# First block of a two-block network: latents' squares taken from PSUM as they are projected, state space outputs transposed per channel block over all eight steps

## The chip, the cores and the metric

The kernel runs on one core of a Trainium2 chip. Its five engines are TensorE (PE, with its weight loads PEld), VectorE (DVE), ScalarE (ACT), GpSimd (POOL) and SyncE (SP), which here only issues DMAs. The metric is the device time of one execution in microseconds; lower is better.

## What is computed

Two blocks run one after the other on 1024 tokens of width 1024. Only the first block is touched by the change. Cut to what matters:

```
x = layer_norm(x)                                   # [1024 tokens, 1024]
z = x @ w_in
xs, gs, cq, ckv, kr, gm = split(z, 512, 512, 256, 128, 64, 512)
ys = s5_branch(xs, ...) * silu(gs)                  # state space model, 32 groups of 16 channels, 64 states
       # y = gelu(scan output + d_skip * xs);  y = y * sigmoid(y @ w_glu + b_glu)
ym = mla_branch(cq, ckv, kr, ...) * silu(gm)        # 4 heads of causal attention
       # q = rms_norm(cq) @ w_uq;  k_nope, v = rms_norm(ckv) @ w_ukv;  rotary on the last 64 of q and on kr
mix = concat(ys, ym) @ w_out
u = alpha * x + mix;  x = layer_norm(u + sigmoid(u @ w_pg) * (p @ w_pp))
```

cq (256 wide) and ckv (128 wide) are the latents. Their RMS norms need, for each token, the sum of squares over the latent's channels. The second block is a dilated attention, a gated linear recurrence and a mixture of 32 experts.

## The kernel before, in words

All matrix products are made in float32 out of three float32r products (high x high, high x low, low x high): `mm3` at L178 to L180, called by `gemm`. A split into high and low is a ScalarE copy (L146, or L150 with a scale) and a VectorE subtraction (L147, L153). `evac` copies a PSUM tile to SBUF, alternating between ScalarE (L139) and VectorE (L141).

The kernel is written with a tile framework. The program text gives instructions in an order of emission; a scheduler at compile time puts them into the queues of the engines, taking whichever is ready in its plan, by the order of emission where several are. On the chip each engine then works through its own queue in order.

`block1` (from L272) begins with the layer norm; x is transposed to xTh and xTl. Then three streams are emitted interleaved by `weave` (L396). Each stream yields its costs as it goes, and `weave` always advances the stream whose sum of costs, divided by the number given with it, is the smallest. The streams:
- `s5_prep` (L774), which makes the state space parameters (costs 84 in all, mostly VectorE work on 128x512 tiles; tables of cosines and sines go to DRAM as d_cos and d_sin, L894 and L895), then `s5_groups` (L899): eight turns over four groups each (8.0 each, 64 in all). A turn makes Q1 on GpSimd and X1p on VectorE (L921 to L923), transposes X1p (L940), runs two input products (L968), a scan on VectorE (L974), output products (L984 to L986, 24 matmuls a turn) and a gelu (L991 to L995), whose result goes to s5y: 128 partitions (blocks of eight tokens), then step t within the block, then 512 channels. The number given is 148.
- The projections x @ w_in: eight chunks of 256 columns, each in four tiles (two column blocks, two halves of the tokens) of 24 matmuls of 128x512, with cost 5.2 each, 32 tiles in all. Results lie channel by token. `g_xs` (L334) handles xs. `g_feat` (L369) handles the latents and the rotary key (copied by `evac` to a tile co, stored to d_c in DRAM at L377) and then the gates gs and gm (`silu2`: a tanh on ScalarE, L331, and a product on VectorE, L332). The number given is 166.4.
- `rest`, then `latent_norms` (L347), then `rotary_tables` (L380); the number given is 180.

`latent_norms` loads each of the six latent tiles (two of cq and one of ckv, in two halves) back from d_c into co (L356), squares it on ScalarE (L357), and sums over the channels on TensorE with four matmuls against a column of ones (L359, eight instructions in the profile). VectorE combines the sums (L364 to L366) and takes the reciprocal root c.lr.

PSUM has eight banks; in this part four tiles G (projections) and four tiles T (all others) of one bank each.

`mla` (L469) comes next. It changes PSUM to G=3, T=3, P=2 and weaves `prep` and `glu`:
- `prep` (L491) loads the latents (ct, L494) and the rotary key (kr, rt) from d_c, broadcasts c.lr by transposes into P (L507), multiplies on VectorE (L510), splits into cnh and cnl, and rotates the key (L487 to L489, L515, L516).
- `glu` (L435) loads the stored gates (gs, L446). For each of the eight steps t it transposes the four 128-channel pieces of s5y into one T tile (L450), splits it into yh and yl at the columns t, t+8, t+16 and so on, and multiplies gs at the same columns (L452). Then eight tiles of y @ w_glu follow (12 matmuls of 128x512 each), each with a tanh (L462) and a product y (L464), stored to DRAM.

After that come the first head's projections (`project`), then attention.

Of the kernel before, what the change touches and what calls it, by code (L numbers as in the profile page):

```python
# [11 lines left out]
FT = mybir.dt.float32  # L12
FR = mybir.dt.float32r
I32 = mybir.dt.int32
AF = mybir.ActivationFunctionType
OP = mybir.AluOpType
# [6 lines left out]
NT = 8  # L23
# [248 lines left out]
def block1(c):  # L272

    tc, nc, I = c.tc, c.nc, c.I
    d = c.dram
    d_xln = c.d_xln = d.tile([S, D], FT, name="d_xln")
    d_c = c.d_c = d.tile([512, S], FT, name="d_c")
# [11 lines left out]
    es1 = ExitStack()  # L289
# [3 lines left out]
    xT = lambda k, sl: (xTh[k // 4][:, k % 4, sl], xTl[k // 4][:, k % 4, sl])  # L293
# [40 lines left out]
    def g_xs(n):  # L334
        w = ch.next()
        for mb in range(2):
            o = stage.tile([128, 8, 128], FT, name="xo")
            for i, h in enumerate(half):
                ps = c.ps()
                c.gemm(ps, [(cols(w[k], mb), xT(k, h)) for k in range(8)])  # L340
                c.evac(o[:, :, 64 * i:64 * i + 64], ps.rearrange("p (n t) -> p t n", t=8))
                yield 5.2
            for g in range(8):
                b, gg = divmod(16 * n + 8 * mb + g, 4)
                nc.scalar.dma_start(d_xu[b, :, gg, :].rearrange("(t c) n -> c t n", t=8), o[16 * g:16 * g + 16])

    def latent_norms():  # L347

        c.lr = c.con.tile([128, 2 * NT], FT, name="lr")
        v = c.sm([128, 2 * NT], name="lv")  # L350
        for i, js in enumerate(((0, 1), (2,))):
            for h in half:
                ps = c.psum_tile("T", [128, 4 * len(js)])
                for j in js:
                    o = stage.tile([128, 512], FT, name="co")
                    nc.sync.dma_start(o, d_c[j * 128:j * 128 + 128, h])  # L356
                    nc.scalar.activation(o, o, AF.Square)  # L357
                    for k in range(4):
                        nc.tensor.matmul(ps[:, 4 * j % 8 + k:4 * j % 8 + k + 1], o[:, k * 128:k * 128 + 128], c.cst[:, 20:21],  # L359
                                         start=True, stop=True)  # L360
                    yield 10.0
                d = v[:, i * NT + h.start // 128:i * NT + h.start // 128 + 4]
                if i == 0:
                    nc.vector.tensor_copy(d, ps[:, 0:4])  # L364
                    nc.vector.tensor_add(d, d, ps[:, 4:8])
                nc.vector.tensor_scalar(d, d if i == 0 else ps, 1.0 / (256, 128)[i], 1e-6, op0=OP.mult, op1=OP.add)  # L366
        c.rsqrt(c.lr, v)

    def g_feat(dst, r0, op):  # L369
        w = ch.next()  # L370
        for h in half:
            for mb in range(2):
                ps = c.ps()
                c.gemm(ps, [(cols(w[k], mb), xT(k, h)) for k in range(8)])
                o = stage.tile([128, 512], FT, name="co")
                op(o, ps)
                nc.sync.dma_start(dst[r0 + mb * 128:r0 + mb * 128 + 128, h], o)  # L377
                yield 5.2

    def rotary_tables():  # L380
        pos = stage.tile([128, S], I32, name="ang", tag="xo")
        k = stage.tile([128, S], FT, name="rk", tag="xo")
        nc.sync.dma_start(pos, bcast_rows(I["positions"], S))
        ang = pos.bitcast(FT)
        nc.vector.tensor_scalar(ang, pos, c.cst[:, 18:19], None, op0=OP.mult)
        yield 4.0
        for h in half:
            c.sincos(stage, ang[:, h], 512, c.rsin[:, h], c.rcos[:, h], "rp", r=ang[:, h], k=k[:, h])
            yield 8.0

    def rest(cost):
        yield cost

    gate = lambda o, ps: silu2(o, ps, 512)

    weave((seq(s5_prep(c, es1), s5_groups(c, es1)), 148.0),  # L396
          (seq(g_xs(0), g_xs(1), g_feat(d_c, 0, c.evac), g_feat(d_c, 256, c.evac),
               g_feat(d_gs, 0, gate), g_feat(d_gs, 256, gate), g_feat(d_gm, 0, gate), g_feat(d_gm, 256, gate)), 166.4),
          (seq(rest(100.0), latent_norms(), rotary_tables()), 180.0))
    wg = ch.next(), ch.next()  # L400
    es1.close()

# [8 lines left out]
def seq(*gens):  # L411
    for g in gens:
        yield from g
# [21 lines left out]
def glu(c, p, w):  # L435

    nc, I = c.nc, c.I
    d_ys = c.d_ys = c.dram.tile([512, S], FT, name="d_ys")
    yh = p.tile([128, 4, S], FR, name="yh")
    yl = p.tile([128, 4, S], FR, name="yl")  # L440
    bg = p.tile([128, 4], FT, name="bg")
    nc.sync.dma_start(bg, I["b_glu"].rearrange("(j p) -> p j", p=128))
    nc.vector.tensor_scalar(bg, bg, 0.5, None, op0=OP.mult)
    gs = p.tile([128, 4, S], FT, name="gs")
    for kb in range(4):
        nc.sync.dma_start(gs[:, kb], c.d_gs[kb * 128:kb * 128 + 128, :])  # L446
    for t in range(8):
        ps = c.psum_tile("T", [128, 4, 128])
        for kb in range(4):
            nc.tensor.transpose(ps[:, kb, :], c.s5y[:, t, kb * 128:(kb + 1) * 128], c.ident)  # L450
        c.split(yh[:, :, t::8], yl[:, :, t::8], ps, scale=0.5)
        nc.vector.scalar_tensor_tensor(gs[:, :, t::8], ps, 0.5, gs[:, :, t::8], op0=OP.mult, op1=OP.mult)  # L452
        yield 0.9
    for mb in range(4):
        for h in range(2):
            hs = slice(h * 512, h * 512 + 512)
            cs = slice((mb % 2) * 128, (mb % 2) * 128 + 128)
            ps = c.ps()
            c.gemm(ps, [((w[mb // 2][k][0][:, cs], w[mb // 2][k][1][:, cs]), (yh[:, k, hs], yl[:, k, hs]))
                        for k in range(4)])  # L460
            th = p.tile([128, 512], FT, name="th", bufs=2)
            nc.scalar.activation(th, ps, AF.Tanh, bias=bg[:, mb:mb + 1], scale=0.5)  # L462
            y = p.tile([128, 512], FT, name="y", bufs=2)
            nc.vector.scalar_tensor_tensor(y, th, 1.0, gs[:, mb, hs], op0=OP.add, op1=OP.mult)  # L464
            nc.sync.dma_start(d_ys[mb * 128:mb * 128 + 128, hs], y)
            yield 2.6


def mla(c, ym, ess, wg):  # L469
# [21 lines left out]
    def prep(q):  # L491
        ct = q.tile([128, 3, S], FT, name="ct")
        for j in range(3):
            nc.sync.dma_start(ct[:, j], c.d_c[j * 128:(j + 1) * 128, :])  # L494
        gq = q.tile([128, 3], FT, name="gq")
        nc.sync.dma_start(gq[:, 0:2], I["q_norm_g"].rearrange("(j p) -> p j", p=128))
        nc.sync.dma_start(gq[:, 2:3], I["kv_norm_g"].rearrange("(j p) -> p j", p=128))
        kr = q.tile([128, S], FT, name="kr")
        nc.sync.dma_start(kr, c.d_c[384:512, :])
        swapped(c.d_c[384:512, :], slice(0, S), nc.sync)  # L500
        yield 0.1
        for i in range(2):
            for h in range(2):
                psb = c.psum_tile("P", [128, 4, 128])
                for mm in range(4):
                    k = i * NT + h * 4 + mm
                    nc.tensor.transpose(psb[:, mm, :], c.lr[:, k:k + 1].to_broadcast([128, 128]), c.ident)  # L507
                hs = slice(h * 512, h * 512 + 512)
                for j in ((0, 1) if i == 0 else (2,)):
                    nc.vector.scalar_tensor_tensor(ct[:, j, hs], ct[:, j, hs], gq[:, j:j + 1],  # L510
                                                   psb.rearrange("p a b -> p (a b)"), op0=OP.mult, op1=OP.mult)
                    c.split(cnh[:, j, hs], cnl[:, j, hs], ct[:, j, hs])
                yield 1
        rotary(kr, slice(0, S))
        nc.vector.tensor_copy(kst[0], kr)  # L515
        nc.vector.tensor_sub(kst[1], kr, f32(kst[0]))  # L516
        yield 1

    with ExitStack() as es2:
        q = c.pool(es2, "mlap")  # L520
        c.psum(G=3, T=3, P=2)
        tc.swap_default_side()
        gp = c.pool(ess, "glu")
        tc.swap_default_side()
        weave((prep(q), 5.0), (glu(c, gp, wg), 28.0))
    ess.close()
    p = c.pool(es, "mlah")
    msk = p.tile([128, 128], FT, name="mskf")
# [471 lines left out]
def weave(*streams, first=False):  # L1000

    st = [[g, t, 0.0] for g, t in streams]
    lead = st[0]
    while st and not (first and lead not in st):
        s = min(st, key=lambda a: a[2] / a[1])
        try:
            s[2] += next(s[0])
        except StopIteration:
            st.remove(s)


class Chunks:
# [9 lines left out]
    def next(self):  # L1022
        self.n += 1
        self.ahead(self.n + 1)
        w, self.w[self.n - 1] = self.w[self.n - 1], None
        return w
# [957 lines left out]
```

## Time and profile before

| | us |
|---|---|
| median of 3 runs | 2118.1 |
| lowest, highest | 2114.16, 2118.48 |
| the profiled execution's own time | 2120.2 |
| its span, first to last instruction | 2118.4 |
| its mean granted TensorE clock | 0.951 |

How to read the profile. All times are from the span's start. A row of the windows gives the stretch, its length, then busy time of PE, PEld, DVE, ACT and POOL with the number of instructions, the granted TensorE clock (1.00 is full), the mean busy share of the DMA engines, and GB/s. A row of the timeline gives start, duration, engine, line, operation and operands, and in brackets how long the engine sat idle before it and what ended that wait. Matmul durations overlap: consecutive ones start closer together than they last. A row of the waits reads "who <- for whom: total, times, longest". A row of the groups ends with busy time, mean duration in ns, and the idle time before. The page by 40 slices of 53 us shows the first block in the slices up to about the 14th; the experts fill the last third.

### The profile page before, as it was taken

What the parts mean: (1) busy time and instruction counts of PE and PEld (TensorE: products, weight loads), DVE (VectorE), ACT (ScalarE), POOL (GpSimd) and SP (SyncE); (2) the same over time, 40 slices, a digit from 0 to 9 for tenths busy, and PEclk for the clock granted to TensorE, in tenths of its full rate; (3) what the DMA queues carried; (4) which work ended last, traced back from release to release, by engine and by line L of the source; (5) the groups of instructions that cost most, each with busy time, mean ns of one, the idle gap of its engine ahead of it and who ended that gap; (6) DMA issues with size and microseconds to landing.
All of it is one profiled execution on the core that took longest, in us unless ns stands there. A gap on an engine that the chain in (4) does not pass through costs nothing.

```text
span 2118.4 us, 34587 instructions
## 1 busy us (share of the span) xinstructions
PE 1937.1 (91%) x13242; PEld 1717.9 (81%) x13242; DVE 1498.3 (71%) x2912; ACT 1030.6 (49%) x1580; POOL 311.9 (15%) x241
## 2 busy tenths in 40 slices
PE   2998995899999979999999999999799999999992
PEld 2776884788999979899999898898688888888881
DVE  7387666676334795757457455668999999999995
ACT  3223333444122234545333223235688888888883
POOL 3014320100000000010010000013322222222211
PEclk9899996999999999999999998899899999999996
DMA  4444533310313131111111011356899999999984
GB/s 172 108 130 146 148 101 122 93 56 31 129 37 110 51 109 46 49 51 46 48 45 45 26 36 35 141 199 235 293 368 376 380 371 372 351 364 367 362 305 169
DMA packets 144374, 350.72 MB, mean 166 GB/s; under 512 B 33888, under 2 KB 87776, under 8 KB 119632
## 3 DMA queue, kind: packets, MB, share of 16 engines
q1 hardware_dynamic: 128160, 325.38, 42.9%
q0 software_dynamic: 11152, 19.97, 3.9%
q10 hardware_dynamic: 4896, 3.15, 0.7%
q8 instruction: 105, 1.72, 0.3%
q14 instruction: 61, 0.50, 0.1%
HBM read 305.81 MB, written 54.01 MB: 170 GB/s over the span
## 4 chain that ended last, share of the span: by engine, by line
PE 38%; issue 24%; DVE 10%; POOL 5%; DMA 3%; ACT 2%; SPq 0%; POOLq 0%; DVEq 0%; ACTq 0%
PE psG L178 8%; PE psG L179 8%; PE psG L180 8%; POOL gates L1840 3%; PE psT L1278 2%; PE psPO L1229 2%; PE psPO L1362 1%; POOL xg L1840 1%; PE psPO L613 1%; PE psSC L1208 1%; PE psSC L1209 1%; DVE Sc L1348 1%; PE psSC L1340 1%; POOL d_acc L1933 1%; DMA wraw<-w_in 1%
## 5 line engine op out<-in xcount | busy, mean ns | idle before, releaser
L1875 DVE TENSOR_TENSOR el<-raw,eh 128x1024 fp32r<-128x1024 f32 x384 | 446.2, 1218 | 32.8 <-ACT eh L1874 31.9
L1874 ACT ACTIVATE eh<-raw 128x1024 fp32r<-128x1024 f32 x384 | 396.0, 1059 | 63.8 <-PE psUU L180 24.4
L178 PE MATMUL psG<-aTh,wh 128*128 128x256 f32 x640 | 188.2, 294 | 0.0
L180 PE MATMUL psG<-aTh,wl 128*128 128x256 f32 x640 | 184.3, 288 | 0.6 <-DVE wl L147 0.6
L179 PE MATMUL psG<-aTl,wh 128*128 128x256 f32 x640 | 184.5, 288 | 0.0
L146 ACT ACTIVATE wh<-wraw 128x512 fp32r<-128x512 f32 (+1 forms) x148 | 91.6, 624 | 187.0 <-PE psG L180 77.2
L178 PE MATMUL psG<-wh,aTh 128*128 128x256 f32 x512 | 147.4, 288 | 0.0
L147 DVE TENSOR_TENSOR wl<-wraw,wh 128x512 fp32r<-128x512 f32 (+1 forms) x148 | 104.9, 716 | 58.9 <-ACT wh L146 48.2
L179 PE MATMUL psG<-wl,aTh 128*128 128x256 f32 x512 | 146.3, 286 | 0.0
L180 PE MATMUL psG<-wh,aTl 128*128 128x256 f32 x512 | 145.6, 284 | 0.0
L178 PEld LDWEIGHTS psG<-aTh,wh 128*128 128x128 f32 x640 | 124.6, 195 | 4.8 <-issue 3.9
L180 PEld LDWEIGHTS psG<-aTh,wl 128*128 128x128 f32 x640 | 124.3, 194 | 2.7 <-issue 1.4
L179 PEld LDWEIGHTS psG<-aTl,wh 128*128 128x128 f32 x640 | 124.7, 195 | 1.4 <-issue 0.9
L180 PE MATMUL psG<-xTh,wl 128*128 128x512 f32 x256 | 105.1, 411 | 3.7 <-DVE wl L147 3.7
L178 PE MATMUL psG<-xTh,wh 128*128 128x512 f32 x256 | 105.6, 413 | 0.4 <-ACT wh L146 0.4
L178 PE MATMUL psY<-eh,hh 128*128 128x512 f32 x256 | 102.3, 400 | 1.7 <-ACT hh L150 1.7
L179 PE MATMUL psG<-xTl,wh 128*128 128x512 f32 x256 | 103.8, 405 | 0.0
L178 PE MATMUL psUU<-eh,xh 128*128 128x512 f32 x256 | 102.6, 401 | 0.0
L178 PE MATMUL psGG<-eh,xh 128*128 128x512 f32 x256 | 101.1, 395 | 0.7 <-ACT xh L146 0.7
L179 PE MATMUL psY<-el,hh 128*128 128x512 f32 x256 | 100.2, 391 | 1.0 <-DVE el L1875 1.0
L180 PE MATMUL psGG<-eh,xl 128*128 128x512 f32 x256 | 100.9, 394 | 0.0
L179 PE MATMUL psGG<-el,xh 128*128 128x512 f32 x256 | 100.3, 392 | 0.0
(539 smaller groups left out, 5305.7 us busy)
## 6 DMA issues: line engine op xcount, KB each, us to landing
raw<-w_gate SPq DMA_DIRECT2D x64, 1024.0 KB
raw<-w_down SPq DMA_DIRECT2D x64, 1024.0 KB
raw<-w_up SPq DMA_DIRECT2D x63, 1024.0 KB
wraw<-w_in SPq DMA_DIRECT2D x52, 256.0 KB
wraw<-w_in SPq DMA_DIRECT2D x68, 128.0 KB
wraw<-w_out SPq DMA_DIRECT2D x32, 256.0 KB
x<-x SPq DMA_DIRECT2D x8, 512.0 KB
d_xln<-x SPq DMA_DIRECT2D x8, 512.0 KB
```

The costliest lines, as they stand in the source:

```text
L146: nc.scalar.activation(h, src, AF.Copy)
L147: nc.vector.tensor_sub(l, src, f32(h))
L178: mm(ps, ah, bh, start=first, stop=False)
L179: mm(ps, ah, bl, start=False, stop=False)
L180: mm(ps, al, bh, start=False, stop=last)
L613: mm(po, v[:, k, :], et[k // 4][:, k % 4, :], start=k == 0, stop=k == qb)
L1208: nc.tensor.matmul(sc[:, ks], QS[j][:, qs], KH[j][:, ks], start=True, stop=False)
L1229: nc.tensor.matmul(po[64 * j:64 * j + 64], v[:, k, (b % 2) * 128 + 64 * j:(b % 2) * 128 + 64 * j + 64], et[j][:, i, :], start=k == 0, stop ...
L1278: nc.tensor.transpose(ps[:, i, :], e[:, (k0 + i) * 128:(k0 + i + 1) * 128], c.ident)
L1840: c.nc.gpsimd.indirect_dma_start(out=dst, out_offset=None, in_=src, in_offset=bass.IndirectOffsetOnAxis(ap=idx, axis=0), bounds_check=src. ...
L1874: nc.scalar.activation(h, src, AF.Copy)
L1875: nc.vector.tensor_sub(l, src, f32(h))
```

## The change

1. The squares of the latents are taken when they are projected. A new generator `g_latents` replaces `g_feat` for the two chunks with d_c. It copies every tile by VectorE, and for the three latent column blocks ScalarE squares the PSUM tile into the tile `th`; the four matmuls against ones for a tile are emitted behind the next tile's projection. The sums are kept in `lv`. `latent_norms` no longer loads or squares anything; it adds the two parts of cq, scales, and takes the root.
2. In the first weave, the number of the state space stream goes from 148 to 160, `rest` from 100 to 120, and the rotary tables come before the norms.
3. `glu` transposes one channel block kb at a time, all eight steps, into a PSUM tile T2 of two banks. yh, yl and gs are written densely; PSUM is read with the steps innermost.
4. PSUM in that part is G=2, T2=2 (two banks each), P=2. `glu` is emitted up to the end of its four blocks before `prep` begins; the rest is woven with 5 and 20.

```
+    lv = c.con.tile([128, 3, NT], FT, name="lv")
+    def squares(j, h, sq):
+        ps = c.psum_tile("T", [128, 4])
+        for k in range(4):
+            nc.tensor.matmul(ps[:, k:k + 1], sq[:, k * 128:k * 128 + 128], c.cst[:, 20:21], start=True, stop=True)
+        nc.vector.tensor_copy(lv[:, j, h * 4:h * 4 + 4], ps)
+    def g_latents(js):
+        w = ch.next()
+        late = None
+        for i, h in enumerate(half):
+            for mb, j in enumerate(js):
+                ps = c.ps()
+                c.gemm(ps, [(cols(w[k], mb), xT(k, h)) for k in range(8)])
+                o = stage.tile([128, 512], FT, name="co")
+                nc.vector.tensor_copy(o, ps)
+                if late:
+                    squares(*late)
+                    late = None
+                if j < 3:
+                    sq = stage.tile([128, 512], FT, name="th", bufs=1)
+                    nc.scalar.activation(sq, ps, AF.Square)
+                    late = j, i, sq
+                nc.sync.dma_start(d_c[j * 128:j * 128 + 128, h], o)
+                yield 5.2
+        if late:
+            squares(*late)
     def latent_norms():
...
-                    nc.sync.dma_start(o, d_c[j * 128:j * 128 + 128, h])
-                    nc.scalar.activation(o, o, AF.Square)
...
+        nc.vector.tensor_add(v[:, :NT], lv[:, 0], lv[:, 1])
+        nc.vector.tensor_scalar(v[:, :NT], v[:, :NT], 1.0 / 256, 1e-6, op0=OP.mult, op1=OP.add)
+        nc.vector.tensor_scalar(v[:, NT:], lv[:, 2], 1.0 / 128, 1e-6, op0=OP.mult, op1=OP.add)
+        yield 1.0
         c.rsqrt(c.lr, v)
+        yield 1.0
...
-    weave((seq(s5_prep(c, es1), s5_groups(c, es1)), 148.0),
-          (seq(g_xs(0), g_xs(1), g_feat(d_c, 0, c.evac), g_feat(d_c, 256, c.evac),
+    weave((seq(s5_prep(c, es1), s5_groups(c, es1)), 160.0),
+          (seq(g_xs(0), g_xs(1), g_latents((0, 1)), g_latents((2, 3)),
...
-          (seq(rest(100.0), latent_norms(), rotary_tables()), 180.0))
+          (seq(rest(120.0), rotary_tables(), latent_norms()), 180.0))
...
-    for t in range(8):
-        ps = c.psum_tile("T", [128, 4, 128])
-        for kb in range(4):
-            nc.tensor.transpose(ps[:, kb, :], c.s5y[:, t, kb * 128:(kb + 1) * 128], c.ident)
-        c.split(yh[:, :, t::8], yl[:, :, t::8], ps, scale=0.5)
-        nc.vector.scalar_tensor_tensor(gs[:, :, t::8], ps, 0.5, gs[:, :, t::8], op0=OP.mult, op1=OP.mult)
-        yield 0.9
+    yield 0
+    for kb in range(4):
+        ps = c.psum_tile("T2", [128, 8, 128])
+        for t in range(8):
+            nc.tensor.transpose(ps[:, t, :], c.s5y[:, t, kb * 128:(kb + 1) * 128], c.ident)
+        ps = ps.rearrange("p t n -> p n t")
+        v = lambda a: a[:, kb].rearrange("p (n t) -> p n t", t=8)
+        c.split(v(yh), v(yl), ps, scale=0.5)
+        nc.vector.scalar_tensor_tensor(v(gs), ps, 0.5, v(gs), op0=OP.mult, op1=OP.mult)
+        yield 1.8
...
-        c.psum(G=3, T=3, P=2)
+        c.psum(G=2, T2=2, P=2)
...
-        weave((prep(q), 5.0), (glu(c, gp, wg), 28.0))
+        turn, pre = glu(c, gp, wg), prep(q)
+        for _ in range(5):
+            next(turn)
+        weave((pre, 5.0), (turn, 20.0))
```

More of the change, by code (lines that the diff above doesn't have):

```diff
@@ L350, in latent_norms @@
         v = c.sm([128, 2 * NT], name="lv")
[L351 to L355, printed above, removed]
-                    nc.sync.dma_start(o, d_c[j * 128:j * 128 + 128, h])
[L357 to L366, printed above, removed]
+        nc.vector.tensor_add(v[:, :NT], lv[:, 0], lv[:, 1])
+        nc.vector.tensor_scalar(v[:, :NT], v[:, :NT], 1.0 / 256, 1e-6, op0=OP.mult, op1=OP.add)
+        nc.vector.tensor_scalar(v[:, NT:], lv[:, 2], 1.0 / 128, 1e-6, op0=OP.mult, op1=OP.add)
+        yield 1.0
         c.rsqrt(c.lr, v)
+        yield 1.0
     def g_feat(dst, r0, op):
```

## The prediction

> **What bounds the kernel now.** I read the page first, then busy time in stretches of 10 us, then the waits, and last the order of the instructions between 60 and 400 us, the only part that the change touches.
>
> ```profile
> PE 1937.1 (91%) x13242; PEld 1717.9 (81%) x13242; DVE 1498.3 (71%) x2912; ACT 1030.6 (49%) x1580; POOL 311.9 (15%) x241
> ```
> ```profile
> 160.00:170.00 10.00, 10.00 (x46) 8.29 (x45) 9.66 (x12) 5.23 (x8) 10.00 (x9) 1.00 0.49 158
> 180.00:190.00 10.00, 4.46 (x15) 3.88 (x16) 3.08 (x6) 3.06 (x4) 0.00 (x0) 0.56 0.54 175
> 340.00:350.00 10.00, 3.11 (x12) 2.14 (x12) 9.59 (x12) 2.98 (x4) 0.00 (x0) 0.50 0.00 0
> 350.00:360.00 10.00, 6.02 (x16) 4.07 (x17) 8.76 (x9) 2.93 (x3) 0.00 (x0) 0.50 0.00 0
> ```
>
> The columns after the stretch are its length, then PE, PEld, DVE, ACT and POOL busy, the granted clock, and DMA. Over the span TensorE is the bound (91%). There are two holes in it: 180 to 190 us, where TensorE is busy less than half and every other engine less than a third, and 340 to 360 us, where VectorE is full and TensorE stands at clock 0.50. The change works on both. Who is waited for:
>
> ```profile
> PE psT L359 <- ACT co L357: 12.3, 3, 9.3
> PE psT L450 <- DVE gs L452: 10.1, 3, 7.9
> ```
>
> The first row is the column sums of the latents' squares, waiting for ScalarE, which squares a tile read back from DRAM. The second is the transposes of the state space outputs, waiting for PSUM buffers that VectorE frees.
>
> **The stage of projections and state space: terms.**
>
> ```profile
> 185.54 1.87 PE L359 MATMUL psT<-cst,co 128*128 128x1 f32 x8 [9.32 <-ACT co L357]
> ...
> 275.35 1.05 PE L359 MATMUL psT<-cst,co 128*128 128x1 f32 x8 [1.84 <-ACT co L357]
> ```
> ```profile
> 186.00:188.00 2.00, 2.00 (x9) 1.90 (x10) 0.29 (x1) 0.00 (x0) 0.00 (x0) 0.50 0.59 175
> 188.00:190.00 2.00, 2.00 (x7) 1.52 (x6) 0.01 (x1) 0.60 (x1) 0.00 (x0) 0.50 0.00 0
> 190.00:192.00 2.00, 2.00 (x7) 1.61 (x6) 1.27 (x2) 0.51 (x1) 0.00 (x0) 0.65 0.23 88
> ```
> ```profile
> 276.00:278.00 2.00, 2.00 (x12) 1.71 (x12) 1.51 (x6) 1.05 (x3) 1.26 (x3) 0.69 0.83 260
> 278.00:280.00 2.00, 2.00 (x7) 1.09 (x6) 1.08 (x4) 0.58 (x2) 0.00 (x0) 0.50 0.88 247
> ```
>
> Removed: the six loads of co from d_c, and with them the 12.3 us of TensorE's waits. After the long wait the clock stays low although TensorE is busy: (1-0.50)x2 twice and (1-0.65)x2 make 2.7 us lost; after the short one (1-0.69)x2 and (1-0.50)x2 make 1.6. Sum of the removed: 12.3+4.3 = 16.6 us. By the Trainium skill ("TensorE: Matmul & The Clock Gate", What's actually happening) the full clock is back after about 3.4 us of steady work; by that the first loss would be 1.7 us instead of 2.7.
>
> The squares themselves stay: six groups of matmuls at 1.05 us (the second row at full clock) move forward among the first sixteen projections. Each is queued behind the next projection's 24 matmuls, so ScalarE has 5.4 us to square a tile:
>
> ```profile
> 104.01 0.39 PE L178 MATMUL psG<-xTh,wh 128*128 128x512 f32 x1
> ...
> 109.45 0.39 PE L178 MATMUL psG<-xTh,wh 128*128 128x512 f32 x1
> ```
>
> The two rows are the first matmuls of k and k+8, so one projection tile takes 5.44 us. The square itself costs ScalarE about as much as the tanh row below (0.60 us) and replaces the square in SBUF: nothing on the path. Its one buffer is shared with the gates' tanh, so a square waits for the sums of the one before, which TensorE has done by then; behind it on ScalarE stand the splits of weights, which are a chunk ahead. The rotary tables only change their place in the order, and their work on VectorE is the same.
>
> Added to VectorE: all eight latent tiles are now copied by it, four of them before by ScalarE, and six small copies.
>
> ```profile
> L141 DVE COPY xo<-psG 128x512 f32<-128x512 f32 x4 | 2.8, 691 | 29.0 <-PE psG L180 28.9
> L141 DVE COPY co<-psG 128x512 f32<-128x512 f32 x4 | 2.7, 680 | 0.0
> L364 DVE COPY lv<-psT 128x4 f32<-128x4 f32 x2 | 0.3, 163 | 7.0 <-PE psT L359 7.0
> ```
>
> 4x0.68+6x0.16 = 3.7 us, at a place where VectorE is full (9.66 of 10 us). It delays the parameters of the state space, and X1p of its first group:
>
> ```profile
> 182.49 0.68 DVE L921 TENSOR_TENSOR X1p<-er,KB 128x512 f32<-128x512 f32 x1
> ```
>
> X1p takes three such operations, so it could stand at 184.5 us now and at 188.2 with the additions. The new weight of that stream (160 for 148) puts the first group behind 84/160x32 = 16.8, so 17 projections, instead of 84/148x32 = 18.2, so 19. TensorE began its long wait at 185.54-9.32 = 176.2 us; two projections earlier (-10.9) and six groups of sums later (+6.3) it would come to the first group at about 172 us and wait 16 us, with fifteen projections queued behind. That is the wait that can take the removed one's place. It shrinks where the scheduler moves projections ahead of a transpose that is not ready, and it does such things:
>
> ```profile
> 325.13 0.49 PE L450 MATMUL psT<-ident,s5y 128*128 128x128 f32 x3
> ...
> 325.46 0.49 PE L507 MATMUL psP<-ident,lr 128*128 128x128 f32 x3
> ```
>
> Of four transposes of one step three run, then those of another stream, emitted later. So the wait lies between 0 and 16 us plus a low clock behind it (up to 3). I take 7.5, somewhat under the middle, because three projections fill the whole of it.
>
> The end of the stage:
>
> ```profile
> 315.15 0.60 ACT L331 ACTIVATE th<-psG 128x512 f32<-128x512 f32 x1 [2.60 <-PE psG L180]
> ...
> 324.68 0.39 PE L985 MATMUL psT<-Q,A 128*128 128x128 f32 x2
> ...
> 324.90 0.39 PE L986 MATMUL psT<-Q,A 128*128 128x128 f32 x2
> ...
> 328.12 0.63 ACT L995 ACTIVATE s5y<-yq 128x512 f32<-128x512 f32 x1 [0.76 <-DVE yq L994]
> ```
>
> The last projection ends at 315.15; the last group's 24 output matmuls (2 in 0.22 us, so 2.7) and its gelu then run alone until 328.75. With the stream emitted ahead, (1-148/160)x32 = 2.4 projections follow it and cover that tail. Last projection in the changed kernel: 315.15-16.6+2.7+7.5 = 308.7 us, between 301 and 320.
>
> **The glu stage: terms.**
>
> ```profile
> 382.00 0.69 DVE L464 SCALAR_TENSOR_TENSOR y<-th,gs 128x512 f32<-128x512 f32 x1 [0.15 <-ACT th L462]
> ```
>
> From the last projection to the end of this last product: 382.69-315.15 = 67.5 us now. VectorE's work in it:
>
> ```profile
> L153 DVE SCALAR_TENSOR_TENSOR yl<-psT,yh 128x512 fp32r<-128x512 f32 x8 | 8.8, 1094 | 2.8 <-ACT yh L150 2.8
> L452 DVE SCALAR_TENSOR_TENSOR gs<-psT,gs 128x512 f32<-128x512 f32 x8 | 8.5, 1090 | 0.0
> L510 DVE SCALAR_TENSOR_TENSOR ct<-ct,gq,psP 128x512 f32<-128x512 f32 x6 | 4.2, 751 | 0.0
> L147 DVE TENSOR_TENSOR cnl<-ct,cnh 128x512 fp32r<-128x512 f32 x6 | 3.9, 697 | 0.0
> L489 DVE TENSOR_TENSOR kr<-kr,rt 128x1024 f32<-128x1024 f32 x1 | 1.2, 1232 | 0.0
> ```
> ```profile
> L150 ACT ACTIVATE yh<-psT 128x512 fp32r<-128x512 f32 x8 | 8.4, 1106 | 9.3 <-PE psT L450 8.7 <-DMA rt<-d_c 0.6
> ```
>
> yl and gs write (gs also reads) with a stride of 8 elements and take 1.09 us for 512 where others take 0.70. Now the writes are dense and the reads from PSUM have a stride of 128 elements over two banks. The nearest row for strided PSUM reads is xo above (stride 8): 691 ns against 680 dense, so free. I take 1.23 us for 1024 elements (the kr row; ScalarE 1.1), with 2.18 as the upper end, the strided price of today. By the Trainium skill ("PSUM — Partial Sum Buffer", Specifications) PSUM has 8-byte cachelines and any non-contiguous pattern slows matmuls significantly; taken over to these reads it speaks against the change, and xo's row does not bear it out.
>
> The second gain is the order: a block now carries one contraction chunk for all tokens, so the first glu matmuls need block 0 and not all eight steps. From the last projection: its tanh and product 1.3; eight transposes at
>
> ```profile
> 350.99 1.09 PE L450 MATMUL psT<-ident,s5y 128*128 128x128 f32 x4 [1.38 <-DVE gs L452]
> ```
>
> 0.27 each, 2.1; yh 1.1; yl 1.2: block 0 is done at +5.8. With two buffers, blocks 2 and 3 wait for gs of blocks 0 and 1, with all glu matmuls queued behind: gs0 +7.0, gs1 +9.5, transposes +11.6, yh +12.7, yl of block 3 at +13.9. Then 0.7 for the first tile's last chunk, seven tiles of half a projection (7x2.72 = 19.0), sixteen transposes of the norms among them (1.8 at 0.11, 4.3 at 0.27 each; I take 2.7), 2 for a low clock, the last tanh and product 1.4: +40. VectorE also does the preparation's products; in the trace
>
> ```profile
> 331.51 1.40 DVE L510 SCALAR_TENSOR_TENSOR ct<-ct,gq,psP 128x512 f32<-128x512 f32 x2
> ...
> 333.81 1.30 DVE L147 TENSOR_TENSOR cnl<-ct,cnh 128x512 fp32r<-128x512 f32 x2
> ```
>
> they came between the first yl. I add 4, hence 44, between 40 and 53 (all 8.1 of ct and cnl and the four of kr, at most 4.9, first). The gate loads now stand ahead of the latents' loads on SP, so gs should be there in time; if not, the two buffers hold everything up, within the same 13 us. One PSUM buffer less for the glu tiles costs nothing while a tanh (0.6) is shorter than a tile (2.7).
>
> Last product: 308.7+44 = 352.7 instead of 382.7, 30 us earlier. Nothing after it waits for a clock time, so the rest shifts. The profiled execution took 2120.2 us, 2.1 over the median, so 2090 by its own time and **2088** for the median.
>
> **Rivals.**
> - TensorE never waits at the first group (last projection at 301): 345, a gain of 38: 2080. For it: the scheduler goes by readiness. Against it: VectorE is late in fact, not in its plan.
> - VectorE keeps the old order, or the strided reads cost 2.18: +53: 361.7, a gain of 21: 2097.
> - No change: the last projection at 320 (the 16 us wait with its low clock), and of the second stage only the dense writes count, 8.8+8.5-8x1.23 = 7.5 of the 67.5 us: 320+60 = 380, a gain of 3: 2115. For it: VectorE is full in both stages. Against it: the covered tail and the order of blocks would both have to fail.
> - Slower: the reads over two banks pay at every element. The place is the eight VectorE reads of 1024, today 1.2 ns an element. It decides from 30/(8x1.024) = 3.7 ns more, 4.9 in all. At 8 ns: 8x1.024x6.8 = 56 us more, less 30: 2144. Against it: no strided row here passes 2.2 ns.
>
> **How the numbers follow.** About 0.2% (4 us, the three runs' spread) can be told from no change. Chances: forecast 0.52, never waiting 0.14, old order 0.20, no change 0.06, slower 0.08; faster is the sum of the first three, 0.86. Low end: 301+40, gain 41.7, with 4 for the spread: 2072. High end: 320+53, gain 9.7, and the same 4: 2112.
>
> **What would show it.** Right: no wait for a square on TensorE; the last tanh of the projections near 309; y's last product near 353; VectorE's yl and gs near 1.23 us; the first glu matmul before the last yl. Wrong: a new long wait at the first group's transposes (L940's place) reaching to 190 us or beyond; yl over 2.2 us; the last product after 375.

## The result, and the profile after

The changed kernel takes 2081.96 us (median of 4 runs, 2080.49 to 2087.04) beside 2116.24 us for the kernel before in the same measurement: a ratio of 0.9841, 95% interval 0.9823 to 0.986, or 34.3 us less. The forecast was 2088 (30 us less), with 2072 to 2112 as its range. The profiled execution took 2080.49 us, with a span of 2078.7. From here on "before" and "after" are the two kernels, and lines behind L345 are numbered as in after: the glu stage's transposes L450 are now L470, its gs L452 is L474, its y L464 is L486; X1p L921 to L923 is L946 to L948, its transposes L940 are L965, the output matmuls L984 to L986 are L1009 to L1011, the last gelu L995 is L1020. The squares' sums are L353, the latents' copies L364, the norms' transposes L529 and their products L532.

First the page's busy times, then the stretches that answer to those of before, then TensorE's waits between 60 and 370 us.

```profile
PE 1922.5 (92%) x13242; PEld 1705.7 (82%) x13242; DVE 1487.3 (72%) x2909; ACT 1023.7 (49%) x1572; POOL 316.5 (15%) x241
```
```profile
140.00:150.00 10.00, 10.00 (x35) 8.32 (x35) 9.70 (x22) 3.12 (x5) 1.35 (x1) 0.56 0.54 159
...
180.00:190.00 10.00, 10.00 (x46) 8.29 (x45) 6.67 (x20) 4.35 (x6) 0.00 (x0) 1.00 0.30 102
190.00:200.00 10.00, 5.35 (x24) 3.76 (x23) 6.54 (x12) 3.84 (x8) 4.05 (x4) 0.66 0.74 223
...
310.00:320.00 10.00, 5.52 (x45) 5.02 (x45) 4.13 (x6) 4.90 (x8) 0.00 (x0) 0.97 0.70 223
...
340.00:350.00 10.00, 10.00 (x47) 8.10 (x46) 7.87 (x13) 3.96 (x7) 0.00 (x0) 1.00 0.47 160
```
```profile
PE psT L965 <- DVE X1p L948: 4.7, 1, 4.7
PE psG L178 <- ACT yh L150: 4.5, 1, 4.5
...
PE psG L180 <- DVE wl L147: 2.7, 1, 2.7
...
PE psT L353 <- ACT th L370: 0.2, 1, 0.2
```

The 12.3 us of waits for squares have become 0.2, and in 340 to 350 us TensorE is full at clock 1.00 where it had 3.11 of 10 us at 0.50. Two smaller holes stand in their place: one for X1p at 190 us, one for yh at 310 us. A third loss shows only in the clock: from 140 to 150 us TensorE is busy throughout, at a mean clock of 0.56. Before had 0.99 there:

```profile
140.00:150.00 10.00, 10.00 (x42) 7.28 (x41) 9.90 (x17) 4.78 (x8) 2.54 (x2) 0.99 0.73 253
```

Both kernels wait here for VectorE's wl (2.73 us until 139.56 in after, 2.35 until 136.90 in before) and go on at half clock. In before that lasts 3.2 us, in after 9.2, so some 3 us more are lost. In after two groups of the squares' sums, matmuls with a single column, run within the first 5 us of the stretch. Of the runs further down, the six with two groups of sums in that place have 8.7 to 10.0 us of half clock there, those with one or none 3.2 to 7.1. That the sums keep the clock low fits all of these; no run changes that alone.

The hole at 190 us in the timeline, with the clock in steps of 2 us:

```profile
190.13 0.69 DVE L946 TENSOR_TENSOR X1p<-er,KB 128x512 f32<-128x512 f32 x1
190.73 0.68 DVE L332 SCALAR_TENSOR_TENSOR co<-th,psG 128x512 f32<-128x512 f32 x1
191.33 0.69 DVE L147 TENSOR_TENSOR wl<-wraw,wh 128x512 fp32r<-128x512 f32 x1
192.88 0.68 DVE L940 TENSOR_TENSOR dg<-dg,ident 16x512 f32<-16x512 f32 x1 [0.86 <-DMA dg<-d_skip]
...
194.79 0.69 DVE L948 TENSOR_TENSOR X1p<-X1p,ctmp 128x512 f32<-128x512 f32 x1
```
```profile
195.63 1.09 PE L965 MATMUL psT<-ident,X1p 128*128 128x128 f32 x4 [4.65 <-DVE X1p L948]
```
```profile
196.00:198.00 2.00, 2.00 (x11) 1.29 (x10) 0.69 (x1) 1.15 (x3) 1.92 (x2) 0.50 0.71 202
198.00:200.00 2.00, 2.00 (x10) 1.59 (x9) 1.26 (x3) 0.59 (x1) 1.71 (x3) 0.50 0.88 219
200.00:202.00 2.00, 2.00 (x15) 1.83 (x15) 1.77 (x5) 0.00 (x0) 0.49 (x2) 1.00 0.73 162
```

TensorE waits 4.65 us, then works at half clock from 195.6 to 200: 2.2 us more. In before, too, dg and its load stood between X1p's operations, and the last one came at 192.76:

```profile
185.61 0.68 DVE L915 TENSOR_TENSOR dg<-dg,ident 16x512 f32<-16x512 f32 x1 [2.44 <-DMA dg<-d_skip]
...
192.76 0.68 DVE L923 TENSOR_TENSOR X1p<-X1p,ctmp 128x512 f32<-128x512 f32 x1
```

So X1p is complete 2.0 us later than before, though its first operation starts 7.6 us later. The second hole, ScalarE's rows first, then TensorE's, then VectorE's:

```profile
309.80 0.60 ACT L331 ACTIVATE th<-psG 128x512 f32<-128x512 f32 x1 [2.53 <-PE psG L180]
313.92 0.63 ACT L146 ACTIVATE wh<-wraw 128x512 fp32r<-128x512 f32 x1 [3.53 <-DMA wraw<-w_uq]
314.46 0.58 ACT L1016 ACTIVATE yq<-psT 128x512 f32<-128x512 f32 x1
...
317.29 0.63 ACT L1020 ACTIVATE s5y<-yq 128x512 f32<-128x512 f32 x1 [0.75 <-DVE yq L1019]
317.82 1.92 ACT L150 ACTIVATE yh<-psT 128x1024 fp32r<-128x1024 f32 x2
```
```profile
312.05 0.39 PE L1011 MATMUL psT<-Q,A 128*128 128x128 f32 x2
312.27 1.91 PE L470 MATMUL psT<-ident,s5y 128*128 128x128 f32 x16
...
318.88 0.49 PE L178 MATMUL psG<-yh,wh 128*128 128x512 f32 x1 [4.48 <-ACT yh L150]
```
```profile
318.86 1.23 DVE L153 SCALAR_TENSOR_TENSOR yl<-psT,yh 128x1024 fp32r<-128x1024 f32 x1 [1.61 <-ACT yh L150]
...
328.42 1.22 DVE L153 SCALAR_TENSOR_TENSOR yl<-psT,yh 128x1024 fp32r<-128x1024 f32 x1
329.55 1.21 DVE L474 SCALAR_TENSOR_TENSOR gs<-psT,gs 128x1024 f32<-128x1024 f32 x1
```
```profile
349.95 0.69 DVE L486 SCALAR_TENSOR_TENSOR y<-th,gs 128x512 f32<-128x512 f32 x1 [1.59 <-ACT th L484]
```

The sixteen transposes of blocks 0 and 1 run before the last gelu, since they don't need its channels; but ScalarE's yh of these blocks stands behind that gelu in its queue, and the gelu behind a split that waits 3.53 us for a weight load. The last product ends at 350.64 us (382.69 before), 32.05 us earlier.

The best mark for the account is the end of the last gelu: 328.75 before, 317.92 after. That is 10.8 us from the stage of projections and state space; from there to the last product it was 53.9 us and is 32.7: another 21.2. The experiments are read by these two marks.

### The profile page after: what moved, and what is told of

It reads as the page before. It is cut to its first block, busy times and chain, and to the rows that moved or that the text cites. A ratio compares the mean times of both kernels' runs of the same rounds, so it can differ in the third digit from the quotient of the medians.

```text
span 2078.7 us, 34559 instructions
## 1 busy us (share of the span) xinstructions
PE 1922.5 (92%) x13242; PEld 1705.7 (82%) x13242; DVE 1487.3 (72%) x2909; ACT 1023.7 (49%) x1572; POOL 316.5 (15%) x241
## 4 chain that ended last, share of the span: by engine, by line
PE 48%; issue 25%; DVE 14%; POOL 5%; DMA 3%; ACT 3%; SPq 0%; POOLq 0%; DVEq 0%; ACTq 0%
PE psG L178 11%; PE psG L179 10%; PE psG L180 10%; POOL gates L1865 3%; PE psT L1303 2%; PE psPO L1254 2%; PE psPO L1387 2%; POOL xg L1865 1%; PE psPO L638 1%; DVE wl L147 1%; PE psSC L1233 1%; DMA wraw<-w_in 1%; PE psSC L1234 1%; PE psT L215 1%; DVE bst L443 1%
## 5 line engine op out<-in xcount | busy, mean ns | idle before, releaser
L180 PE MATMUL psY<-eh,hl 128*128 128x512 f32 x256 | 100.6, 393 | 0.0
```

Of the source, the lines that this page charges most:

```text
L180: mm(ps, al, bh, start=False, stop=last)
```

## The experiments

The theory: the sums' waits are worth some 10 us, and the glu stage some 20, half from dense writes and half from the order (a block's matmuls start before the last block is split). The rivals: one half does nearly all, or the numbers of the weave don't count, or the strided access doesn't.

**Each half alone.** First the latents with the weave's numbers, and the glu stage as before; then the glu stage alone.

```
# e1: glu(), psum(G=3, T=3, P=2) and weave((prep(q), 5.0), (glu(c, gp, wg), 28.0)) as before
# e2: g_latents, latent_norms and the first weave as before
```

> The latents' squares from PSUM and the new numbers of the first weave, with the glu stage as before. My theory (two halves that add up): TensorE does not wait for a square any more, the last state space output comes about 11 us earlier (318 instead of 329 us), and the glu stage keeps its 54 us from there to its last product, which ends near 372 us: some 11 us faster than before, near 2105 us. Rival (the re-read only covered a VectorE that is late anyway): TensorE waits for the first group's X1p instead, the state space ends within 4 us of before, and the time is within 4 us of it.

> The glu stage of the changed kernel (blocks of one contraction chunk, dense writes, two-bank tiles), with the latents read back and the old numbers in the first weave. My theory: the last state space output stays near 329 us, the glu stage takes 33 us from there to its last product instead of 54, so the last product ends near 362 us: some 21 us faster than before, near 2095 us. Rival (only the dense writes count, and the order of blocks helps only where the gate loads come early): 8 us faster, near 2108 us, last product near 375 us.

Measured: 2106.11 us, ratio 0.9946 (0.993 to 0.9963), and 2101.43, 0.992 (0.9899 to 0.994), beside 2118.11 for before. One row from the waits of the first, one from the second:

```profile
PE psT L469 <- DVE gs L471: 10.3, 3, 8.1
```
```profile
PE psT L359 <- ACT co L357: 11.1, 3, 8.3
```

Each half keeps the other's wait. The last products are at 376.2 and 361.5 us: 6.5 and 21.2 earlier, together 27.7 of the 32.05. The first half moves the last gelu by 9.8 us (to 318.9), but the old glu stage gives 3.3 of that back. The times fell by 12.0 and 16.7 us, which does not follow the last products closely: from the last product to the end the two profiled executions took 1728.1 and 1739.5 us (1735.7 in before, 1728.1 in after), though nothing is changed there.

**The weave's numbers as before, the rest as after.**

```
-    weave((seq(s5_prep(c, es1), s5_groups(c, es1)), 160.0),
+    weave((seq(s5_prep(c, es1), s5_groups(c, es1)), 148.0),
-          (seq(rest(120.0), rotary_tables(), latent_norms()), 180.0))
+          (seq(rest(100.0), rotary_tables(), latent_norms()), 180.0))
```

> The changed kernel with the old numbers in the first weave (148 and 100 for 160 and 120). My theory (the scheduler goes by readiness, the numbers only break ties, and the tail of the last group was not covered by projections in the changed kernel either): last product within 3 us of the changed kernel's 351 us, time 2079 to 2086 us. Rival (the numbers set how much of the tail is covered and how long TensorE waits at the first group): last product 8 us or more later, time 2090 us or more.

Measured: 2089.76 us, ratio 0.9864 (0.9843 to 0.9885). The last tanh of the projections starts at 308.0, 1.8 us earlier than in after, the last gelu ends at 321.4, 3.5 later, and the last product at 356.1, 5.5 later. It lies between the two expectations: the numbers are worth about 5 us of the 32.

**Blocks with strided writes.**

```
-        ps = ps.rearrange("p t n -> p n t")
-        v = lambda a: a[:, kb].rearrange("p (n t) -> p n t", t=8)
+        v = lambda a: a[:, kb].rearrange("p (n t) -> p t n", t=8)
```

> The changed kernel with its blocks of one contraction chunk, but PSUM read densely and yh, yl and gs written with a stride of 8 elements, as before the change. My theory (VectorE's chain of yl and gs is the path between the first and the last block): yl and gs take 2.18 us for 1024 elements instead of 1.22, seven of them lie ahead of the last yl, and yh's two on the path take 2.2 instead of 1.0, so the last product comes 7 to 9 us later and the time is near 2090 us. Rival (the order of blocks is the gain, and the matmuls hide the writes): less than 3 us later, 2082 to 2085 us.

Measured: 2091.4 us, ratio 0.987 (0.985 to 0.9891). The rows of gs and of y as groups by source line; the columns are the count, the least, median and greatest ns, and the first and last start:

```profile
L473 DVE SCALAR_TENSOR_TENSOR gs<-psT,gs x4: 2030/2054/2106, 326.5 to 337.8; 128x1024 f32<-128x1024 f32 x4
```
```profile
L485 DVE SCALAR_TENSOR_TENSOR y<-th,gs x8: 683/688/699, 340.4 to 359.5; 128x512 f32<-128x512 f32 x8
```

gs takes 2.05 us, and yl 2.04, with strided accesses to SBUF (the writes, and the reads of yh and of the gates) and dense PSUM reads, against 1.22 with dense SBUF and strided PSUM: the price is SBUF's side. By the Trainium skill ("Advanced Engine Details and Errata", Memory Cachelines) an access that meets a new 16-byte line of SBUF each time pays a penalty; a stride of 32 bytes does that, and the rows agree. From the last gelu (320.6) to the last product (360.2) it is 39.5 us, 6.8 more than after. My theory came true, a little above its range: the last product is 9.5 us later than after's, of which 2.7 us stand ahead of the last gelu.

**The old weave of prep and glu, with blocks; and the new order, step by step.**

```
# e5
-        turn, pre = glu(c, gp, wg), prep(q)
-        for _ in range(5):
-            next(turn)
-        weave((pre, 5.0), (turn, 20.0))
+        weave((prep(q), 5.0), (glu(c, gp, wg), 28.0))
# e9: the loop over t of before in glu(), G=3, T=3, and
-        for _ in range(5):
+        for _ in range(9):
```

> After, with the glu stage and the attention's preparation written in the old order (one weave from the start, no five steps of the glu stage ahead). Theory: what orders the four blocks' transposes, splits and gate products is when the state space outputs and the gates come, not where they stand in the program, so the last product of the glu stage stays within 2 us of 350.6 us and the time within 3 us of after's. Rival: without the five steps ahead the preparation's work on VectorE and its loads on SP stand before the splits, yl and gs come 5 to 10 us later, the last product is at 356 to 361 us, and the time is about 2088 to 2093 us (this stage's share of what the second half brings).

> After, with the glu stage's transposes, splits and gate products step by step as before the change (strided writes, eight PSUM tiles of four blocks), but all of them ahead of the attention's preparation, as after has it. Nothing is left out. The run with the old weave lost 15 us of this stage because the preparation's products stood before the gate products on VectorE. Theory: order and form add up. VectorE has 16 products of about 1.09 us (17.4 us) before the first matmul of the glu stage, since each of those reads all eight steps, so the last product is at 358 to 365 us (350.6 after, 376.2 with the old stage in the old order), the time 2090 to 2096 us. Rival: the order matters only for four blocks, and step by step the stage stays as long as with the old order: last product at 372 to 378 us, time 2103 to 2108 us.

Measured: 2100.62 us, ratio 0.9905 (0.9888 to 0.9923), and 2099.39, 0.9916 (0.99 to 0.9931). My theory for the first fell, and its rival was too small. One wait of TensorE and VectorE's rows behind it:

```profile
PE psT L470 <- DVE gs L474: 6.4, 1, 6.4
```
```profile
324.38 1.41 DVE L532 SCALAR_TENSOR_TENSOR ct<-ct,gq,psP 128x512 f32<-128x512 f32 x2 [2.55 <-DMA gq<-q_norm_g]
...
326.84 3.22 DVE L147 TENSOR_TENSOR cnl<-ct,cnh 128x512 fp32r<-128x512 f32 x2
329.99 2.05 DVE L532 SCALAR_TENSOR_TENSOR ct<-ct,gq,psP 128x512 f32<-128x512 f32 x3
...
337.37 2.34 DVE L474 SCALAR_TENSOR_TENSOR gs<-psT,gs 128x1024 f32<-128x1024 f32 x2
```

The first gs starts at 337.37, and at 322.61 in after. Both PSUM buffers of the transposes are held until then, the last two blocks wait, and with them all glu matmuls but the first ones of blocks 0 and 1. The edit changes two things at once: VectorE is busy with the preparation without a gap from 326 us on, and SP issues the gates' loads at 324.34 instead of 315.34, behind the preparation's. How the 13 us divide between them was not tried. In the other run the rows of y, and the first gs:

```profile
L484 DVE SCALAR_TENSOR_TENSOR y<-th,gs x8: 681/688/693, 346.6 to 366.8; 128x512 f32<-128x512 f32 x8
```
```profile
328.53 3.09 DVE L472 SCALAR_TENSOR_TENSOR gs<-psT,gs 128x512 f32<-128x512 f32 x3 [4.21 <-DMA kr<-d_c]
```

That lies between the two expectations: the last product, at 367.5 us, is 2.5 us beyond the theory's upper end and 4.5 us ahead of the rival's range, and the time 3.4 us beyond the theory's. VectorE stood idle 4.2 us for loads there. From the last gelu to the last product, with the latents as in after everywhere (in us):

| | old weave | glu's products first |
|---|---|---|
| step by step, strided in SBUF | 57.2 | 48.0 |
| by block, strided in SBUF | | 39.5 |
| by block, dense in SBUF | 45.7 | 32.7 |

Order alone brings 9.2, blocks alone 11.5, both 24.5. Of the 15.3 that blocks bring in the new order, 6.8 are the dense accesses and 8.5 the rest. Chunks that can be multiplied before the last is there, fewer turns of the buffers and the 4.2 us for loads in the run step by step can all have part in these 8.5; they were not separated.

**The latents' copies on both engines, and the groups further ahead.** The next two were also tries at a better version; the third is the changed kernel again.

```
# e6 and e7, in g_latents
-                nc.vector.tensor_copy(o, ps)
+                c.evac(o, ps)
# e7 also: 172.0 for 160.0, rest(130.0) for rest(120.0)
```

> After, with the copies of the projected latents made by ScalarE and VectorE in turn, as before the change, instead of all on VectorE. The prediction charged VectorE 2.72 us for the four extra copies and took their whole delay of X1p to the first group. Theory: X1p of the first group starts 2 to 4 us earlier than 190.1 us, TensorE's wait for it (4.65 us) shrinks to 1 to 3 us, and the time falls by 1 to 4 us. Rival: the delay is from the squares' results or from ScalarE's share of the preparation, X1p starts within 1 us of 190.1 us, and the time is the same within 1 us or longer.

> As the run before, and with the weave's numbers raised once more in the direction of the change: 172 for the state space stream (160 after, 148 before) and a rest of 130 (120 after, 100 before). What is looked for is a better version: the last group's outputs were to be covered by projections and were not (309.6 to 312.1 us, behind the last projection at 309.8 us). Theory: the groups move ahead of the projections, the last group's outputs end at least 3 us before the last projection's tanh, the transposes of the blocks begin within 4 us of it, and the last product comes 3 to 8 us earlier than 350.6 us, the time 2074 to 2079 us. Rival: TensorE then reaches the first group sooner and waits longer for X1p (8 us or more instead of 4.65 us), and what the tail gives is lost there: the time within 3 us of after's or above it.

> The changed kernel once more, unaltered, beside the three others on the same chip: 2078 to 2086 us, and the last product of the glu stage within 1 us of 350.6 us. What the time from the glu stage to the end does between two profiled executions of the same kernel shows how far the 5 us that are gained behind the changed stages are its own.

Measured on one chip: 2079.75 us, ratio 0.982 (0.98 to 0.9839); 2081.71, 0.9821 (0.9802 to 0.9839); and the changed kernel 2084.91, 0.9838 (0.9825 to 0.9851). In the first of them:

```profile
184.98 0.69 DVE L946 TENSOR_TENSOR X1p<-er,KB 128x512 f32<-128x512 f32 x1
```
```profile
PE psT L965 <- DVE X1p L948: 5.4, 1, 5.4
```
```profile
L486 DVE SCALAR_TENSOR_TENSOR y<-th,gs x8: 676/685/2507, 327.0 to 345.6; 128x512 f32<-128x512 f32 x8
```

X1p starts 5.1 us earlier than in after (4.2 earlier than in the repeat) for 2.72 us of copies taken from VectorE, and yet TensorE's wait did not shrink (5.4 after 4.65): TensorE comes there 5.8 us earlier too. Its waits for VectorE's wl and for a square are 1.7 us together instead of 2.9, and two groups of sums that ran at half clock in after run at full clock here, behind that stretch; the rest was not taken apart. So half of my theory fell. The last product is at 346.3 us, 4.3 before after's and 4.6 before the repeat's. The medians differ by 5.2 us but the intervals overlap, so this is the best version seen, not one established as better.

With the groups further ahead the last projection's tanh starts at 309.6, the last gelu ends at 312.1, where it had ended at 312.3, and the last product at 347.3. The groups moved ahead of the last projections as meant, by 1 us and not by 3, but the last gelu did not come earlier: the projections only came later. In the repeat of after, the last product is at 350.9 us, 0.3 from the first execution, and the span 2083.7 against 2078.7. Two executions of the same program differ by 5 us behind the changed part, so the difference between 32.05 us at the last product and 39.7 in the spans is of that size and is not put down to the change. The medians, 34.3 us apart, lie nearer to the last product.

**The gates' loads from ScalarE's queue.** In after SP issued the preparation's loads first:

```profile
313.49 1.27 SPq L516 DMA_DIRECT2D ct<-d_c  x3
314.81 0.43 SPq L461 DMA_DIRECT2D bg<-b_glu  x1
315.34 2.53 SPq L465 DMA_DIRECT2D gs<-d_gs  x4
```
```
# e10, on e6; e11 the same on e7
-    nc.sync.dma_start(bg, ...)
+    nc.scalar.dma_start(bg, ...)
-        nc.sync.dma_start(gs[:, kb], ...)
+        nc.scalar.dma_start(gs[:, kb], ...)
```

> The run with the latents copied by both engines, and with the five loads of the glu stage (bias and gates) issued from ScalarE's queue instead of SP's, where the attention's loads went ahead of them. Looked for is a better version. Theory: the first gate product comes 1 to 3 us earlier than 318.25 us, the transposes of the third block follow it, and the last product comes 1 to 3 us earlier than 346.3 us, the time 2076 to 2079 us. Rival: both sets of loads share the DMA engines, which were busy to 0.90 in 310 to 320 us, or the issues hold up ScalarE's yh, and nothing is gained: last product at 346 us or later.

> The same edit of the loads on the version with the groups first (172 and 130), where the waits for the bias and the gates (1.83 and 0.45 us) stood right behind the covered tail. Theory: with the loads earlier the cover pays: last product at 342 to 345 us (347.3 without the edit), and the time 1 to 4 us below the run before. Rival: as there; and then the last product stays at 346 to 348 us.

Measured: 2086.2 us, ratio 0.9856 (0.9836 to 0.9875), and 2085.79, 0.9852 (0.9833 to 0.9871); last products at 354.0 and 350.6, later by 7.7 and 3.3 us than without the edit. ScalarE in the first:

```profile
314.03 8.53 ACTq L465 DMA_DIRECT2D gs<-d_gs  x4
322.67 1.94 ACT L150 ACTIVATE yh<-psT 128x1024 fp32r<-128x1024 f32 x2 [8.64 <-DMA kr<-d_c]
```

The rival came true in both, and the second lost more than it said. In the first the four issues held ScalarE for 8.5 us, and yh stood behind them, 10.5 us later than without the edit; in the second they took 2.67 us, and yh came 3.2 us later. By the Trainium skill ("Trainium Kernel Development and Optimization", Key Constraints) issuing from several engines only saves issue time, since all use the same DMA engines; in the first run not even that was saved, since the same four issues had taken 1.99 us on SP.

**The latents behind the gates.** This takes the latents' squares, sums and roots away from the time ahead of X1p.

```
# on e6, with the weight chunks in the same order
-          (seq(g_xs(0), g_xs(1), g_latents((0, 1)), g_latents((2, 3)),
-               g_feat(d_gs, 0, gate), g_feat(d_gs, 256, gate), ...
+          (seq(g_xs(0), g_xs(1), g_feat(d_gs, 0, gate), g_feat(d_gs, 256, gate),
+               g_latents((0, 1)), g_latents((2, 3)), ...
```

> The version with the latents copied by both engines, with the order of the projections changed: the four gate chunks of the glu stage (d_gs) first and the latents with their squares behind them. Nothing is left out. In after VectorE made the reciprocal roots of the latents' sums (14 small products, 4.2 us, 170.7 to 185.2 us) ahead of the first group's X1p; the prediction did not count that move. Here they, the sums' copies and the latents' copies stand behind it. Theory: the roots are part of what made X1p late, so X1p of the first group starts 3 to 6 us earlier than 185.0 us, TensorE's wait for it (5.4 us) shrinks to 0 to 3 us, and the last product comes 2 to 5 us earlier than 346.3 us, the time about 2075 to 2078 us. Rival: X1p waits for ScalarE's exponentials and sines and for the load of d_skip, and the gates' tanh now stands among these with its table loads (1.28 us each): X1p no earlier or later, the wait 5 us or more, and the time the same or up to 10 us longer.

Measured: 2098.65 us, ratio 0.9902 (0.9886 to 0.9919); last product at 361.2.

```profile
185.20 0.68 DVE L946 TENSOR_TENSOR X1p<-er,KB 128x512 f32<-128x512 f32 x1
```
```profile
PE psT L965 <- DVE X1p L948: 8.5, 1, 8.5
```
```profile
155.13 1.28 ACT L331 ACT_TABLE_LOAD   x1
...
157.05 1.28 ACT L243 ACT_TABLE_LOAD   x1
...
159.51 1.28 ACT L331 ACT_TABLE_LOAD   x1
```

X1p is no earlier (185.20 against 184.98) and its wait is longer. ScalarE's tanh and the sines of the parameters now take turns, with a table load at each, and VectorE waits 6.3 us for ScalarE between 150 and 186 us instead of 2.2. The theory is not borne out; whether the roots cost anything where they stand in after stays open, since the table loads came in their place. The wait for X1p is only a part of the 14.9 us that the last product lost: the glu stage lost some too, with waits of 5.3 us for yl instead of 1.1. That was not followed further.

## Why the prediction was right or wrong

- **The removed waits** (12.3 us and a low clock): right. TensorE waits 0.2 us for a square, and the half alone moved the last gelu by 9.8 us. What the forecast did not count is the half clock around the moved sums, 140 to 149 us, some 3 us more than before; it charged the sums nothing beyond the 1.05 us that each group took before.
- **VectorE's additions before the first X1p** (3.7 us): too small. The step that failed is "X1p takes three such operations, so it could stand at 184.5 us now and at 188.2 with the additions". Its first operation moved by 7.6 us, to 190.13, and the three took 5.35 us instead of 2.0, since a gate product, two splits and the product with dg, which waits for a load, stand among them. The trace before already spoke against 184.5: dg stood behind its load until 185.61 there, and X1p was complete at 193.4. The run with the copies on both engines shows that the copies count for more than their own time. The 14 small products of the roots, 4.4 us, had also moved ahead of X1p, which the step did not count; their share was not separated.
- **TensorE's wait at the first group** (0 to 16 us, 7.5 taken with the low clock): 4.65 and 2.2 make 6.9. That the size fits is luck, since both times whose difference it is were far off: X1p was complete at 195.5 us, not 188.2, and TensorE came at 191, not 172. The new number did not bring the first group forward: 463 matmuls of projections, a little over 19 projections, ran ahead of it, and 454 in before, where 17 projections were forecast. The forecast also began at the wait of 176.2 us, behind which before had 19 more of these matmuls ahead of the first group, and it had no half clock at 140 us. Last projection: 309.8 against 308.7.
- **"2.4 projections follow it and cover that tail"**: wrong. The output matmuls ran behind the last projection, until 312.4 us, and the gelu to 317.9. The 2.7 us that the sum had for them ahead of the last projection were not there; the half clock at 140 us cost about as much, so 309.8 is near the forecast by luck. In the run with the higher numbers the cover brought nothing: TensorE has the same work, and the last gelu ends at the same time.
- **1.23 us for 1024 elements, PSUM strides free**: right, 1.22. The forecast's sentence from the Trainium skill on PSUM's lines is not borne out for these reads, and with it the rival that ended slower falls. The dense writes were put at 7.5 us of VectorE's work; on the path they are 6.8.
- **The glu stage, 44 us from the last projection**: 40.8. The last yl ended 19.8 us behind the last projection's tanh instead of 13.9, mostly the uncovered tail; but from there to the last product it took 21.0 instead of 25.8, since the norms' transposes and some of the glu matmuls ran ahead of it and the clock was full. The 4 us for the preparation's products among the blocks were not needed: the first of them starts at 330.68, behind the last gs.
- **"The gate loads now stand ahead of the latents' loads on SP"**: wrong, as the rows of SP show. It cost little: VectorE stood idle 1.1 us for the bias ahead of block 1's yl, which ended at 322.5, and gs followed at once.
- **The rival of the old order on VectorE** was the right danger and had too low a price: 9 us there, 13.0 when it was brought about. What kept it off is the emission of glu's five steps ahead, not the blocks.

So both stages were worth about what the forecast said (5.4 us up to the last projection, 6.4 forecast; 26.7 behind it, 23.5 forecast), but that the sum came within 2 us is partly luck. In the first stage a missing term and an uncounted one cancel; in the second, behind the last projection, the last yl came 5.9 us later than forecast, the rest took 4.8 less, and 4 us were not needed.

## What to carry to other kernels

Where two streams share an engine and one of them frees the buffers that TensorE waits for, emit that one's loads and products first: here the order was worth 13 us and the dense accesses 7. Keep SBUF dense and read PSUM strided, not the other way round. The tail was not shortened here by putting other work behind it; look for what the last link itself waits for, such as a split queued ahead of it that waits for a load. In the run with the copies on both engines that split did not stand in the way, and the last gelu ended 3.4 us behind the last output matmul instead of 5.5; no run changed that alone. Matmuls with a single column right behind a wait of TensorE are worth moving away (read from the traces here, not tried alone).

## What the runs showed of the hardware that was not expected

- The issue of the same four loads of 512 KB took 1.97 us (the repeat of after) to 4.21 us (the weave's old numbers) on SP, and 2.67 and 8.53 us on ScalarE's queue, always with other loads in flight; on ScalarE compute stands behind that.
- VectorE reads PSUM with a stride of 512 bytes over two banks at 1.22 us for 1024 elements, while the same with strided SBUF and dense PSUM reads costs 2.05.
- After a wait of some 2.5 us TensorE's half clock lasted 3.2 us where matmuls of 512 columns followed (before), and 9.2 where two groups of matmuls with a single column stood among them (after), though the profile shows TensorE busy in both stretches.
